# Low parts of the weight strips formed by an accumulating DMA instead of a subtraction on VectorE

## The chip, the cores and the metric

The kernel runs on one core of a Trainium2 chip. The metric is the device time of one execution in microseconds (us), the median of the runs. The core has TensorE (matrix products, PE; its weight loads are listed as PEld), VectorE (DVE), ScalarE (ACT), GpSimd (POOL) and SyncE (SP, which here only issues transfers), and 16 DMA engines that all queues share.

## The reference, cut to what matters

One step of a two-layer network on 512 latent and 128 context tokens with 1024 features, in float32. Layer 0 mixes by differential attention and a spatial gate, layer 1 by a gated convolution; after each mixer stands a squared-ReLU MLP with 4096 hidden features, and a layer norm follows every block. For this change one formula is enough:

```python
def sq_relu_mlp(h, w1, w2):
    return jnp.square(jax.nn.relu(h @ w1)) @ w2
```

Every `h @ w` of the model is such a product. The kernel forms each one from split operands: with w = w_hi + w_lo and h = h_hi + h_lo, each part having 12 significant bits, `h @ w` is w_hi h_hi + w_hi h_lo + w_lo h_hi, three passes of the array that add up in float32.

## The kernel before, in words

The activations are kept with features on the 128 partitions and the 640 tokens along the free axis, in two halves of 320 columns. The weights of all large products are cut on the host into 188 strips of 128x1024 float32 (512 KB), in the order of use, in the DRAM tensor `wall`.

`prepare(i)` (lines 84 to 91) brings strip i into shape: SyncE loads it into a staging tile `raw` (four buffers, line 59, shared with the modulation's weights), a tile `w` of two parts is taken from a pool, and `split` (lines 64 to 67) fills it: ScalarE casts the strip to the 12-bit type into part 0 (line 66), VectorE subtracts part 0 from the strip into part 1 (line 67). `split` is also used for activations; those calls are not touched. The tile `w` comes from a pool of four buffers (`w1p`, line 60) in layer 0's mixer; later from this pool and one of three (`w2p`, line 788) in turn, seven in all. `strip()` (line 98) hands out the next strip and calls `prefetch` for the strip three further on (`LOOKAHEAD`, line 42). It also runs some steps of a background generator: sections of the modulation (`mod_section`, line 150; `mod_products`, line 171), whose weights pass through the same staging tiles.

`mm3` (lines 71 to 74) issues the three passes. A strip gives 48 products of 128x128 with 320 columns; in the token-major projections (`token_major`, line 385) two strips together give 120 products of 256 columns, and the strip is there the moving operand, so its low part is read by the second product. The strips in order: 0 to 3 queries and keys of two heads, used at the start tile by tile as the input arrives; 4 to 7 values (token-major); 8 to 11 queries and keys; 12 to 15 the gate; 16 to 19 the gate's values (token-major); 20 to 27 the output projection; 28 to 91 the MLP; 92 to 123 layer 1's mixer; 124 to 187 its MLP. `run_block` (line 700) uses strips one by one ("alt") or, where a norm follows or precedes, six strips with the first half of the tokens and then the same six with the second ("ab").

The order of the instructions on each engine is made when the program is built: a planner replays the program with a table of costs, and puts each instruction in its engine's queue when, by that table, its inputs and a buffer are there. On the chip each queue runs strictly in that order, and semaphores do the waiting. GpSimd has in all eleven instructions in the trace, all of them clears of tiles; two of them come late, `minus_mean` (line 797) and `zb` (line 1038), each taking memory that earlier tiles give up.

Of the kernel before, what the change touches and what calls it, by code (L numbers as in the profile page):

```python
"""One inference step of the hybrid backbone on one core.

Everything on the chip is kept feature-major ([feature on partitions, token on the free axis]),
512 latent tokens then 128 context tokens, so that products chain without transposes, the adaLN
terms are per-partition scalars and the depthwise convolution slides along the free axis.

Float32 products: each operand is split exactly into hi + lo of 12 significant bits (float32r), and
hi*hi + hi*lo + lo*hi are three passes of the array that accumulate in float32 in PSUM.
"""
# [12 lines left out]
ALU = mybir.AluOpType  # L22
AX = mybir.AxisListType
PSUM = bass.MemoryType.PSUM

P = 128
# [16 lines left out]
AHEAD = 36  # products of the out projection before the spatial gating, which they then alternate with  # L43
WARM = (10, 18, 12)
# The attention's pieces in the order in which they are issued. By two blocks of queries: a, b the
# softmax of each, V the values; by head: C, X the same for the context, N the norm's scales, M the
# norm; F half a strip of the projections.
# [5 lines left out]
def build(ctx, tc, io):  # L53
# [9 lines left out]
    # ---------------------------------------------------------------- helpers  # L63
    def split(hl, src):
        """hl[:, 0] = hi, hl[:, 1] = lo of src (a float32 tile in SBUF)."""
        S.copy(out=hl[:, 0], in_=src)  # L66
        V.tensor_tensor(out=hl[:, 1], in0=src, in1=hl[:, 0].bitcast(F32), op=ALU.subtract)  # L67
# [3 lines left out]
    def mm3(ps, lhs, rhs, first, last):  # L71
        """ps += lhs.T @ rhs; lhs(i), rhs(i) give part i (0 hi, 1 lo)."""
        for n, (i, j) in enumerate(PASSES):
            nc.tensor.matmul(ps, lhs(i), rhs(j), start=first and n == 0, stop=last and n == 2)  # L74

    # ------------------------------------------------- the stream of weights
# [7 lines left out]
    def prepare(i):  # L84
        raw = raw_tile()
        stream["dma"] = nc.sync.dma_start(out=raw, in_=io["wall"][i])
        pool = wpools[stream["slot"] % len(wpools)]
        stream["slot"] += 1
        w = pool.tile([P, 2, D], F32R, name="w")
        split(w, raw)  # L90
        stream["w"][i] = w
# [6 lines left out]
    def strip(ahead=True, behind=None):  # L98
        """The next strip; loads those ahead, and a round of the background, behind the instruction given."""
        i = stream["next"]  # L100
        stream["next"] += 1
        if ahead:
            prefetch(i + LOOKAHEAD)
        with nullcontext() if behind is None else tc.issue_after(behind.ins):
            step_background()
        return stream["w"].pop(i)

    # -------------------------------------------------------------- constants
# [10 lines left out]
    def start_load(out, in_):  # L119
        """The loads that the start needs, in this order."""  # L120
        with in_turn():
            start_dma.append(nc.sync.dma_start(out=out, in_=in_))
# [11 lines left out]
    # ------------------------------------------------------------------ adaLN  # L134
# [5 lines left out]
    # [stream, section, tile]; sections: shift, scale + 1, gate, twice  # L140
# [9 lines left out]
    def mod_section(layer, sec, ps, rows):  # L150
        """A section of a layer's modulation for both streams: KT steps and a last one."""
        for k in range(KT):
            raw = raw_tile()
            nc.sync.dma_start(out=raw, in_=io[f"wmod{layer}"][k * P:(k + 1) * P, sec * D:(sec + 1) * D])
            for b in range(2):
                j = 2 * (k % 2) + b
                nc.tensor.matmul(ps[32 * j:32 * j + 32, :], cs[:, k, :], raw[:, b * 512:(b + 1) * 512],  # L157
                                 start=k < 2, stop=k >= KT - 2)
            yield
        msb = rows()  # L160
        S.copy(out=msb, in_=ps)
        p2 = ps[:, 0:16].rearrange("p (f i) -> p f i", f=4)
        for f in range(4):
            nc.tensor.matmul(p2[:, f, :], msb[:, f * P:(f + 1) * P], sel, start=True, stop=True)
        pv = p2.rearrange("p f (b i) -> p b f i", b=2)
        mod_finish([(modT[layer][:, i, sec, :].rearrange("p (b f) -> p b f", b=2), pv[:, :, :, i],
                     bmod[layer][:, sec * KT:(sec + 1) * KT].rearrange("p (b f) -> p b f", b=2), sec in (1, 4))
                    for i in range(2)])
        yield

    def mod_products(layer, sec, rows):
        """A section of a layer's modulation on VectorE, from the transposed weights: KT steps."""
# [21 lines left out]
    def behind(gen, rate):  # L194
        """Run rate steps of gen with every strip that is fetched."""
        background.append([gen, rate])
# [20 lines left out]
    def mod_products_start(raws, ps):  # L217
        """A feature tile of layer 0's first shift and scale: four partial sums, for both streams."""
# [5 lines left out]
    def mod_finish_start(f, ps, rows):  # L224
        """Their sum, features on partitions."""
# [8 lines left out]
    # The input of a block: x * (1 + scale) + shift, split.  # L234
    def modulate(hl, x, sc, sh, segs, tmp_pool, c0):
        """hl[:, :, cols] from x (its columns start at c0); sc(i), sh(i): [P, 1] by stream."""
# [10 lines left out]
    # =================================================== phase 1: mixer of layer 0  # L247
# [15 lines left out]
    # The start: q and k of two heads, tile by tile as the modulation's weights arrive.  # L263
# [39 lines left out]
    with tc.manual_schedule(engines={mybir.EngineType.PE}):  # L303
        start_ps[3, 0] = mmp.tile([P, HALF], F32, name="mm")

        def keep_warm(n):
            """Products that nobody reads, while there are no others: the array's clock falls when it idles."""
            for _ in range(n):
                nc.tensor.matmul(start_ps[3, 0][:, 0:P], mean_w, mean_w, start=True, stop=True)  # L309
# [39 lines left out]
    def proj_halves(w):  # L349
        """One 128-feature strip over all tokens: the two halves' PSUM tiles, in turn."""  # L350
# [14 lines left out]
    def rotary(kind, h, f):  # L365
        """The rotary on the latent columns, split."""
# [18 lines left out]
    def token_major(consume, tile_, between=None):  # L385
        """[128 tokens, 256 features] for the five token tiles, twice; strips: k quadruples."""
# [24 lines left out]
    def softmax_pair(q, k, qc, kc, nkeys):  # L411
        """(p1 - lam p2) * 2^-E for 128 queries (columns qc) over keys kc..kc+nkeys."""
# [34 lines left out]
    def values(h, pair, es):  # L447
        """The head's values for two blocks of queries."""
# [20 lines left out]
    def context_values(h, e):  # L469
        """The same for the context's queries, which attend to the context's keys alone."""  # L470
# [10 lines left out]
    def attention_scales(h):  # L481
        """RMS norm over the head's 128 features: each token's -2 / sqrt(mean square + EPS)."""
# [30 lines left out]
    def g_consume(t, block, ps):  # L513
        """Layer norm within each group, per token."""
# [38 lines left out]
    # lambda, and a power of two that keeps the attention's output in range  # L553
# [55 lines left out]
    def gates(tag, width):  # L609
        """Two of u's strips, kept in float32."""  # L610
# [7 lines left out]
    def fillers():  # L618
        """Products that run while a softmax does."""
# [40 lines left out]
    def mm_tile(shape):  # L660
        """A bank for products, of the six in turn."""
# [10 lines left out]
    def accumulate(m, half, ps, gt, scale_x=False):  # L672
        """xa += gate * ps (the first time for layer 0: alpha * xa + gate * ps)."""
# [17 lines left out]
    def products(w, nk, srcs, half, m0=0):  # L691
        """Strip w's product with srcs for one half of the tokens."""
# [7 lines left out]
    def run_block(items, order, norm=None):  # L700
        """Strips and what is done with them by half; 'alt' strip by strip, 'ab' one half first. Then norms of a half."""
# [16 lines left out]
    # --- out projection of layer 0: attention's features, then the gated ones  # L718
# [22 lines left out]
    def oa_steps():  # L741
        """The first strips of the projection, product by product."""
# [13 lines left out]
    # spatial gating: mix each 128-token chunk along its tokens, between the projection's products  # L756
# [30 lines left out]
    # ======================================================= phase 2: the rest  # L787
# [12 lines left out]
    # parameters that a norm's outputs are formed with  # L800
    def norm_params(layer, which):
        """alpha * (g, b) for the residual; g', b' for the next block's input."""
# [14 lines left out]
    def rsqrt(v):  # L817
        """-2 / sqrt(v + EPS)."""
# [14 lines left out]
    def tally(m, half):  # L833
        """Moments of xa's half about the mean of its first two tiles, which is taken off xa, tile by tile."""
# [44 lines left out]
    def final_norm(half, pr):  # L879
        """The last norm, from the moments."""  # L880
# [42 lines left out]
    def layer_norm(half, pr, hs):  # L923
        """Norm over the features of xa's half; xa <- residual, hs[k] <- next input, split."""
# [25 lines left out]
    def norms(layer, which):  # L950
        """The next block's input, what normalizes a half into it, and what completes the residual."""
# [25 lines left out]
    def ff(layer, hs, residual, following, then=None):  # L977
        """Squared-ReLU MLP of a layer, from hs into xa; residual() completes xa."""
# [56 lines left out]
    # --- layer 1's mixer: y = W_out(b * conv3(c * x))  # L1035
# [64 lines left out]
# ---- host side: layouts only  # L1100
def _strip(w, m):
    """[p, k, c] of a 1024-row matrix's 128-column block m."""
# [118 lines left out]
```

## Time and profile before

| | |
|---|---|
| runs | 1494.41 and 1495.93 us, median 1495.17 us |
| profiled execution, first to last instruction (span) | 1490.6 us |
| its own time | not listed apart from the span; the runs lie 3.8 to 5.3 us above it |
| TensorE busy | 1477.9 us (99%) |
| VectorE busy | 894.6 us (60%) |
| ScalarE busy | 558.2 us (37%) |
| GpSimd busy | 2.2 us |
| DMA | 161.85 MB, 109 GB/s in the mean |

How to read it: busy time is the union of an engine's instructions; the share is of the span. A busy TensorE is pipelined work, one product of 320 columns starting every 148 ns (624.8 us for 4224). "Waited" is idle time of an engine in front of an instruction, put down to what released it last.

### The profile page before, as it was taken

What the parts mean: (1) busy time and instruction counts of PE and PEld (TensorE: products, weight loads), DVE (VectorE), ACT (ScalarE), POOL (GpSimd) and SP (SyncE); (2) the same over time, 40 slices, a digit from 0 to 9 for tenths busy, and PEclk for the clock granted to TensorE, in tenths of its full rate; (3) what the DMA queues carried; (4) which work ended last, traced back from release to release, by engine and by line L of the source; (5) the groups of instructions that cost most, each with busy time, mean ns of one, the idle gap of its engine ahead of it and who ended that gap; (6) DMA issues with size and microseconds to landing.
All of it is one profiled execution on the core that took longest, in us unless ns stands there. A gap on an engine that the chain in (4) does not pass through costs nothing.

```text
span 1490.6 us, 24292 instructions
## 1 busy us (share of the span) xinstructions
PE 1477.9 (99%) x10126; PEld 1426.1 (96%) x10126; DVE 894.6 (60%) x1726; ACT 558.2 (37%) x1032; POOL 2.2 (0%) x11
## 2 busy tenths in 40 slices
PE   8999999999999999999999999999999999999998
PEld 7779888999999999999999999999999999999997
DVE  3656855789986596586557534449533433433456
ACT  3435655346613213213317522216712312312313
POOL 0000000000000000000000000000000000000000
PEclk9999999999999999999999999999999999999999
DMA  9762015322664274275211322212222222222102
GB/s 353 197 206 78 31 36 199 112 88 71 211 227 142 85 226 142 78 222 154 86 54 59 102 83 71 80 35 86 86 85 73 83 71 71 85 72 71 58 1 71
DMA packets 50877, 161.85 MB, mean 109 GB/s; under 512 B 8400, under 2 KB 12112, under 8 KB 50640
## 3 DMA queue, kind: packets, MB, share of 16 engines
q1 hardware_dynamic: 50768, 160.31, 33.9%
q8 instruction: 79, 1.29, 0.4%
q14 instruction: 30, 0.25, 0.0%
HBM read 157.13 MB, written 3.15 MB: 108 GB/s over the span
## 4 chain that ended last, share of the span: by engine, by line
PE 95%; DVE 2%; DMA 1%; ACT 1%; issue 0%; SPq 0%; ACTq 0%; DVEq 0%
PE mm L74 86%; PE sc L425 2%; PE mod L157 1%; PE po L74 1%; PE mm L751 1%; DMA raw<-wmod 1%; PE pt L459 1%; PE ms L221 1%; PE mm L309 0%; PE st L940 0%; DVE w L67 0%; DMA mraw<-wstart 0%; PE ss L488 0%; PE rb L504 0%; PE st L927 0%
## 5 line engine op out<-in xcount | busy, mean ns | idle before, releaser
L74 PE MATMUL mm<-hn,w 128*128 128x320 f32 x4224 | 624.8, 310 | 0.5 <-ACT hn L241 0.5
L74 PEld LDWEIGHTS mm<-hn,w 128*128 128x128 f32 x4224 | 620.4, 188 | 2.9 <-ACT hn L241 1.7
L74 PE MATMUL mm<-hid,w 128*128 128x320 f32 x3072 | 453.4, 309 | 0.0
L74 PEld LDWEIGHTS mm<-hid,w 128*128 128x128 f32 x3072 | 451.2, 188 | 0.5
L66 ACT CAST w<-raw 128x1024 fp32r<-128x1024 f32 x188 | 196.6, 1047 | 368.6 <-PE mm L74 283.5
L67 DVE TENSOR_TENSOR w<-raw,w 128x1024 fp32r<-128x1024 f32 x188 | 229.4, 1222 | 172.2 <-ACT w L66 170.9
L677 DVE SCALAR_TENSOR_TENSOR xa<-mm,modT,xa 128x128 f32<-128x128 f32 (+2 forms) x264 | 108.0, 435 | 152.5 <-PE mm L74 152.4
L989 ACT ACTIVATE relu<-mm 128x320 f32<-128x320 f32 x128 | 55.7, 436 | 236.3 <-PE mm L74 236.3
L74 PE MATMUL mm<-hin,w 128*128 128x320 f32 x576 | 97.7, 315 | 0.3 <-DVE w L67 0.2
L991 DVE TENSOR_TENSOR relu<-relu,mm 128x320 f32<-128x320 f32 x128 | 61.5, 483 | 54.9 <-ACT hid L990 54.9
L74 PEld LDWEIGHTS mm<-hin,w 128*128 128x128 f32 x576 | 85.1, 188 | 6.1 <-issue 4.3
L178 DVE SCALAR_TENSOR_TENSOR unused<-raw,srows 128x1024 bf16<-128x1024 f32 x56 | 68.4, 1221 | 33.2 <-DMA raw<-wmodT 33.1
L74 PEld LDWEIGHTS mm<-w,hin 128*128 128x128 f32 x480 | 59.4, 190 | 16.7 <-issue 15.2
L178 DVE SCALAR_TENSOR_TENSOR raw<-raw,srows 128x1024 f32<-128x1024 f32 x56 | 68.2, 1219 | 0.5
L74 PE MATMUL mm<-w,hin 128*128 128x256 f32 x480 | 65.6, 288 | 0.4 <-DVE w L67 0.4
L992 DVE TENSOR_TENSOR hid<-relu,hid 128x320 fp32r<-128x320 f32 x128 | 62.5, 491 | 3.2
L990 ACT ACTIVATE hid<-relu 128x320 fp32r<-128x320 f32 x128 | 60.2, 472 | 2.0
L74 PE MATMUL mm<-mx,w 128*128 128x320 f32 x384 | 57.5, 310 | 0.0
L74 PEld LDWEIGHTS mm<-mx,w 128*128 128x128 f32 x384 | 56.5, 188 | 0.5 <-DVE mx L67 0.2
L74 PE MATMUL mm<-mix,w 128*128 128x320 f32 x288 | 43.2, 311 | 0.0
L74 PEld LDWEIGHTS mm<-mix,w 128*128 128x128 f32 x288 | 42.5, 188 | 0.3
L240 ACT ACTIVATE hf<-xa,np 128x192 f32<-128x192 f32 (+1 forms) x72 | 36.8, 560 | 4.5 <-DVE xa L944 4.2
(218 smaller groups left out, 937.0 us busy)
## 6 DMA issues: line engine op xcount, KB each, us to landing
raw<-wall SPq DMA_DIRECT2D x188, 512.0 KB, 3.6
raw<-wmodT SPq DMA_DIRECT2D x56, 512.0 KB, 3.7
raw<-wmod SPq DMA_DIRECT2D x24, 512.0 KB, 5.2
mraw<-wstart SPq DMA_DIRECT2D x16, 512.0 KB, 10.6
x<-xT SPq DMA_DIRECT2D x4, 640.0 KB, 10.0
xa<-xT SPq DMA_DIRECT2D x8, 320.0 KB, 4.5
yT<-xa SPq DMA_DIRECT2D x8, 320.0 KB, 2.3
srows<-silu_rows SPq DMA_DIRECT2D x1, 1024.0 KB
```

The lines of the kernel that those rows point to most:

```text
L66: S.copy(out=hl[:, 0], in_=src)
L67: V.tensor_tensor(out=hl[:, 1], in0=src, in1=hl[:, 0].bitcast(F32), op=ALU.subtract)
L74: nc.tensor.matmul(ps, lhs(i), rhs(j), start=first and n == 0, stop=last and n == 2)
L157: nc.tensor.matmul(ps[32 * j:32 * j + 32, :], cs[:, k, :], raw[:, b * 512:(b + 1) * 512], start=k < 2, stop=k >= KT - 2)
L178: V.scalar_tensor_tensor(out=out, in0=raw, scalar=1.0, in1=rows[:, i], op0=ALU.mult, op1=ALU.mult, accum_out=modT[layer][:, i, sec, f:f + 1])
L240: S.activation(out=hf[:, a - lo:b - lo], in_=x[:, a - c0:b - c0], func=AF.Identity, scale=sc(i), bias=sh(i))
L425: nc.tensor.matmul(scs[i][:, b, 0:n], q[r, x, qc:qc + P], k[r, y, kc + b * n:kc + (b + 1) * n], start=m == 0, stop=m == 2)
L677: V.scalar_tensor_tensor(out=xa[:, m, a:b], in0=ps[:, a - COLS[half][0]:b - COLS[half][0]], scalar=gt(i), in1=xa[:, m, a:b], op0=ALU.mult, ...
L989: S.activation(out=r, in_=ps, func=AF.Relu)
L990: evac.append(S.activation(out=hid[m][:, 0, c0:c1], in_=r, func=AF.Square))
L991: V.tensor_tensor(out=r, in0=r, in1=ps, op=ALU.mult)
L992: lows[0] = V.tensor_tensor(out=hid[m][:, 1, c0:c1], in0=r, in1=hid[m][:, 0, c0:c1].bitcast(F32), op=ALU.subtract)
```

## The change

For the strips from 4 on, `prepare` no longer calls `split`. ScalarE writes the cast of the strip into part 0 as before, and then the strip times -1, cast in the same way, into part 1: the negated high part. Then GpSimd issues a DMA that reads the strip a second time from DRAM and adds it onto part 1, which leaves strip - high part, the low part. The first four strips keep the old form.

```diff
         w = pool.tile([P, 2, D], F32R, name="w")
-        split(w, raw)
+        if i < 4:
+            split(w, raw)
+        else:
+            S.copy(out=w[:, 0], in_=raw)
+            S.mul(out=w[:, 1], in_=raw, mul=-1.0)
+            G.dma_start(out=w[:, 1], in_=io["wall"][i], accum_op=ALU.add)
         stream["w"][i] = w
```

The rest of the diff takes away comments and texts only.

## Rows read from the trace of the kernel before

**Rows 1.** Busy times of the whole run: us, share of the span, instructions.
```profile
PE 1477.9 (99%) x10126; PEld 1426.1 (96%) x10126; DVE 894.6 (60%) x1726; ACT 558.2 (37%) x1032; POOL 2.2 (0%) x11
```

**Rows 2.** Windows: us; PE, PEld, DVE, ACT, POOL busy (instructions); PEclk, DMA share, GB/s.
```profile
300.00:400.00 100.00, 99.48 (x667) 98.02 (x666) 92.50 (x184) 60.33 (x114) 0.00 (x0) 1.00 0.34 107
...
400.00:740.00 340.00, 340.00 (x2320) 340.00 (x2319) 243.39 (x437) 91.41 (x146) 0.00 (x0) 1.00 0.50 154
740.00:1480.00 740.00, 740.00 (x5001) 734.72 (x5000) 366.87 (x628) 250.68 (x432) 1.21 (x2) 1.00 0.22 70
...
1200.00:1300.00 100.00, 100.00 (x684) 100.00 (x683) 38.62 (x63) 26.47 (x42) 0.00 (x0) 1.00 0.23 74
```

**Rows 3.** Timeline at 1200 us: start us, length us, engine, line, what [idle before <-releaser].
```profile
1200.19 1.05 ACT L66 CAST w<-raw 128x1024 fp32r<-128x1024 f32 x1 [5.30 <-PE mm L74]
...
1201.27 1.23 DVE L67 TENSOR_TENSOR w<-raw,w 128x1024 fp32r<-128x1024 f32 x1 [0.41 <-ACT w L66]
...
1207.23 1.05 ACT L66 CAST w<-raw 128x1024 fp32r<-128x1024 f32 x1 [5.99 <-PE mm L74]
```

**Rows 4.** Windows, tile `w` alone: PE, PEld, DVE, ACT (instructions), clock, DMA.
```profile
0.00:231.00 231.00, 133.92 (x841) 117.88 (x841) 24.25 (x20) 20.92 (x20) 1.00 0.46 147
0.00:740.00 740.00, 627.66 (x4166) 603.43 (x4167) 110.74 (x91) 95.08 (x91) 1.00 0.46 147
0.00:1200.00 1200.00, 1084.19 (x7249) 1056.20 (x7250) 189.00 (x155) 162.10 (x155) 1.00 0.38 120
```

**Rows 5.** Waits, whole run: who waited for whom, us in total, times, longest us.
```profile
PE mm L74 <- DVE w L67: 0.6, 2, 0.4
...
PEld mm L74 <- DVE w L67: 1.9, 3, 0.8
...
SPq L86 <- DVE w L67: 797.7, 144, 26.2
```

**Rows 6.** Groups: busy us, mean ns of one | idle us before, releasers.
```profile
L66 ACT CAST w<-raw 128x1024 fp32r<-128x1024 f32 x188 | 196.6, 1047 | 368.6 <-PE mm L74 283.5
L67 DVE TENSOR_TENSOR w<-raw,w 128x1024 fp32r<-128x1024 f32 x188 | 229.4, 1222 | 172.2 <-ACT w L66 170.9
...
L676 ACT ACTIVATE xa<-xa 128x320 f32<-128x320 f32 x8 | 3.7, 464 | 1.9 <-DMA xa<-xT 1.9
```

**Rows 7.** DMA issues: count, KB each, median us from issue to landing.
```profile
raw<-wall SPq DMA_DIRECT2D x188, 512.0 KB, 3.6
...
mraw<-wstart SPq DMA_DIRECT2D x16, 512.0 KB, 10.6
```

**Rows 8.** Timeline about 55 us: strips 4 and 5, and the products that use them.
```profile
53.27 1.05 ACT L66 CAST w<-raw 128x1024 fp32r<-128x1024 f32 x1
...
54.85 1.07 ACT L66 CAST w<-raw 128x1024 fp32r<-128x1024 f32 x1
...
55.79 0.43 SPq L86 DMA_DIRECT2D raw<-wall  x1
...
57.09 0.28 PE L74 MATMUL mm<-w,hin 128*128 128x256 f32 x1
57.75 2.42 PE L74 MATMUL mm<-w,hin 128*128 128x256 f32 x18 [0.38 <-DVE w L67]
```

**Rows 9.** Timeline about 295 us: products of strip 22 on, casts of strips 25 to 27.
```profile
293.74 18.50 PE L74 MATMUL mm<-mix,w 128*128 128x320 f32 x125
293.94 1.05 ACT L66 CAST w<-raw 128x1024 fp32r<-128x1024 f32 x1 [10.03 <-PE mm L751]
...
297.96 1.05 ACT L66 CAST w<-raw 128x1024 fp32r<-128x1024 f32 x1
...
299.93 1.06 ACT L66 CAST w<-raw 128x1024 fp32r<-128x1024 f32 x1 [0.93 <-DVE mix L67]
```

**Rows 10.** GpSimd's two late instructions, whole run.
```profile
231.15 0.21 POOL L797 MEMSET minus_mean<- 128x128 f32 x1 [229.79 <-DVE mix L67]
741.16 1.21 POOL L1038 MEMSET zb<- 128x643 f32 x2 [509.81 <-DVE raw L178]
```

## The prediction

> **What bounds the kernel now.** I read busy time first, then the stretches, then the waits, then single instructions. In the busy times TensorE is busy for 1477.9 of 1490.6 us [rows 1], so all its idle time together is 12.7 us, 0.85% of the span. In the windows it is busy for over 99% of every stretch shown, at granted clock 1.00, the higher level of 2.4 GHz [rows 2]. So nothing that this change touches can be worth much on the fast side: it can only take away idle time of TensorE, or add some.
>
> The strips come in faster than they are used. A strip is 48 matmuls. In the stretch at 1200 us the high-part cast starts every 7.04 us (1200.19, 1207.23), each time after ScalarE had waited over 5 us for a TensorE product [rows 3]: the cast waits for a buffer that TensorE has just finished reading, so the buffers are full. Counting up to 1200 us, 7249 products have read strips, of which 96 are the excess of the eight token strips (60 instead of 48), so (7249-96)/48 = 149 strips are used up while VectorE has formed 155 low parts [rows 4]: six strips lie ready, about 6 x 7.04 - 2.5 = 39 us of lead. At 740 us it is (4166-96)/48 = 84.8 against 91, again six; at 231 us, with only four buffers and half of the token strips behind, (841-48)/48 = 16.5 against 20, 3.5 strips. TensorE's waits say the same from the other side: for the low parts it waited 0.6 us as a matmul and 1.9 us as a weight load in the whole run [rows 5].
>
> **The change part by part.** 188 strips pass through line 90; strips 0 to 3 keep the old form, so 184 change.
>
> Removed: 184 subtractions on VectorE at 1222 ns [rows 6], 225 us of its 894.6. TensorE waited 2.5 us for them in all. Of this the matmul's 0.38 us at 57.75 [rows 8], with the weight load in front of it about 1 us, belongs to strip 4, which stands below; at most 1.5 us is left to win.
>
> Added on ScalarE: 184 multiplications by -1 of 128x1024. Not in the trace; the cast of the same size takes 1047 ns, and a multiplication of 128x320 takes 464 ns [rows 6], close to a cast or copy of its width. I take 1.05 us each, 193 us, so ScalarE goes from 558 to about 751 us, half of the span. What lies in front of it: in the fullest stretch shown it is at 60% [rows 2], and the some 14 strips of 100 us add 15. It delays chains in the attention (strips 4 to 19) by up to 1.05 us each, 17 us if each one reached TensorE; but VectorE, which is in the same chains, loses 1.22 us each, so -4 to +8 us are the ends and 0 is the value.
>
> Added on DMA: 184 transfers of 512 KB from GpSimd's queue. The trace has neither an accumulating transfer nor any transfer from that queue. Its latency T from issue to landing is bounded below by the median of the same strip loaded by SyncE, 3.6 us, and above by the median of the 512 KB loads of the crowded start, 10.6 us [rows 7]; I take 6 us, nearer to the first, since it moves the same strip but must also read what it adds to. The low part of a strip then stands 1.05 + T = 7 us after its high part, where it stood 1.3 us (1201.24 to 1202.50) [rows 3] to 3.4 us (54.32 to at most 57.75, strip 4) [rows 8] after it.
>
> The Trainium skill, "DMA: Bandwidth & Descriptors", section "Anatomy of one DMA — SWDGE (gpsimd) path", fits such a transfer as about 2.0 us plus its bytes at 436 GB/s, by estimate 3.2 us here; that fit is for a copy, and no run here shows it yet. By it the loss at the strips 4 and 5 below would be 2.0 us instead of 4.8.
>
> Where this lies on the path: with 39 us of lead, nowhere in the steady stages. It shows where a strip is used soon after its buffer comes free.
>
> Strips 4 and 5, at the first products of the values. Their casts start at 53.27 and 54.85 us, and TensorE starts on strip 4 at 57.09 and already waits for its low part, until 57.75 [rows 8]. Strip 5 is the 13th product of a tile, 57.75 + 11 x 0.134 = 59.2 us. After the change: cast to 54.3, multiplication to 55.4 for strip 4; for strip 5 cast to 56.9, multiplication to 58.0, landing 58.0 + T = 64.0. TensorE runs its products in the order written, so it is late by 64.0 - 59.2 = 4.8 us (2.4 with T = 3.6, 9.4 with T = 10.6). Queued behind are only TensorE's own later products; GpSimd has nothing else to do there.
>
> Strips 25 to 27, in the output projection, where six strips are used in one half and only four buffers exist. The products start at 293.74 and a half strip is 24 x 0.148 = 3.53 us, so strips 25, 26, 27 are needed at 304.3, 307.8, 311.4; their casts start at 293.94, 297.96, 299.93 [rows 9]. With the multiplication right behind, T may be 8.3, 7.7 and 9 us before TensorE waits. At T = 6 it costs nothing, at 10.6 some 3 us, not added up because each strip's delay covers the next.
>
> The loads. SyncE's queue waited 797.7 us for VectorE's subtraction, 144 times [rows 5]; this is the staging buffer coming free. It is now freed by ScalarE, somewhat earlier in the dense stages; the loads move earlier by a microsecond or two, which the lead makes worthless. GpSimd's queue: two clears wait there, until 231.15 and 741.16 us [rows 10], and an accumulating transfer put behind one waits with it. Around both, three and six strips lie ready [rows 4], over 20 and 39 us, so zero; if the planner puts a clear earlier than it can run, it costs the part of that time beyond the lead.
>
> Sum against the profiled execution: 1490.6 + 4.8 - 1.5 + 0 = 1493.9 us of span. The runs' median lies 1495.17 - 1490.6 = 4.6 us above the span, for what stands around it; so 1498.5 us.
>
> **The rivals.**
>
> Slower, the 16 DMA engines fill. The stretch from 1200 to 1300 us shows what a plain strip costs: share 0.23 with one strip each 7.04 us, 1.62 us of all engines. From 400 to 740 us the second layer's modulation is loaded beside the strips and the share is 0.50 [rows 2]. Let an accumulating strip cost m plain ones. Then that stage needs 0.50 + 0.23 m: full at m = 2.2, and when (0.23 m - 0.5) x 340 us exceeds the 39 us of lead, from m = 2.7, TensorE waits. At m = 3.5 it loses 104 - 39 = 65 us there and, with 0.22 + 0.81 = 1.03 in the 740 us behind, some 20 more: 1580 us; at m = 4 about 1700. For it: the transfer reads the strip, reads its target and writes it. Against it: two reads and one write suggest m about 2, and reads and writes may overlap.
>
> The Trainium skill, same page, section "Rules for kernel authors", says that an accumulating transfer reads its destination and writes it later; no row here shows how long that holds an engine, and m above is bounded by the arithmetic of the rows alone.
>
> Slower, GpSimd or the transfer takes longer than 7.04 us each, one at a time. Then the lead runs out whatever the share; at 9 us it is 184 x 1.96 = 360 us, 1855 us. For it: the trace has no transfer issued by GpSimd, so its time per issue is unbounded here. Against it: a SyncE issue takes 0.43 us when nothing blocks it [rows 8], a sixteenth of the 7.04 us that a strip has.
>
> No loss at the start: the planner puts other ready products (scores, modulation) ahead of strip 4's, and only the 1.5 us of waits go: 1493 to 1494 us. For it: both kinds of products run in that stretch anyway. Against it: the before kernel already waited there.
>
> The change cannot be 2% faster: that is 30 us, and TensorE idles for 12.7.
>
> **How the numbers follow.** Hidden but for the start, 1498.5 us: 0.63, own range 1491 to 1512 (T from 3.6 to 10.6 gives -2.4 to +4.6 and 3 more, ScalarE -4 to +8, not all at once). No loss at the start: 0.10. DMA engines full: 0.20. Serial transfers: 0.07. The range goes from 1490 to 1560 us: it takes in the first two, and the engine rival up to about m = 3.3, and leaves out less than 0.2. About 2% is what counts as a difference here (1465 to 1525 us is no change). Slower by over 2% needs m above 3.0 or the serial case: 0.17 + 0.07 = 0.24; faster 0.01; the rest, 0.75, within.
>
> **What would show it.** Right: VectorE near 670 us and ScalarE near 751; 184 activations of about 1.05 us on the new line; about 96 MB from a second queue; a gap of TensorE of 2 to 9 us about 57 to 64 us whose releaser is that transfer; TensorE's full busy time from 70 us on; DMA share in 400 to 740 us below 1. Wrong: gaps of TensorE spread over 400 to 740 us with the share at 1 (engines full), a regular period above 7.04 us in the last stages (serial), or a lead at 1200 us below six strips.

## The result, and the profile after

The changed kernel takes 1538.68 us (two runs, 1538.54 and 1538.83), the kernel before 1495.17 us; the ratio is 1.0303 [1.0285, 1.0320] (these two medians alone give 1.0291, 43.5 us). The time lies in the range that was given, but not near the likeliest value of 1498.5 us. Its profiled execution spans 1536.7 us, 46.1 more than the profiled one before.

The page of after, busy times and the two DMA queues (packets, MB, share of the 16 engines):

```profile
PE 1492.6 (97%) x10126; PEld 1437.3 (94%) x10126; DVE 692.1 (45%) x1542; ACT 726.2 (47%) x1216; POOL 161.4 (11%) x195
...
q0 software_dynamic: 26496, 96.48, 34.2%
q1 hardware_dynamic: 50768, 160.31, 33.0%
```

The first line splits the loss. TensorE's idle time is 1536.7 - 1492.6 = 44.1 us, where it was 12.7 [rows 1]: +31.4. Its busy time is 14.7 us longer with the same 10,126 products; most of that is products at half the clock (below). The two add up to the 46.1 us. VectorE (692) and ScalarE (726) came out near the 670 and 751 that the working had; neither is the bound.

The changed lines by groups (line, engine, what, busy us, mean ns | idle before), and the DMA issues (KB each, median us from issue to landing). The lines of the change are 93 to 95 here, and later lines stand five further on:

```profile
L94 ACT ACTIVATE w<-raw 128x1024 fp32r<-128x1024 f32 x184 | 193.3, 1053 | 0.0
L93 ACT CAST w<-raw 128x1024 fp32r<-128x1024 f32 x184 | 192.3, 1045 | 339.2 <-PE mm L74 165.6 <-DMA raw<-wall 132.7 <-issue 30.5
L95 POOL DMA_DIRECT2D w<-wall x184 | 159.2, 865 | 1317.8 <-ACT w L94 1084.1 <-DVE s L374 54.9 <-PE sc L430 52.9
```
```profile
raw<-wall SPq DMA_DIRECT2D x188, 512.0 KB, 4.7
w<-wall POOLq DMA_DIRECT2D x184, 512.0 KB, 7.2
raw<-wmodT SPq DMA_DIRECT2D x56, 512.0 KB, 5.4
raw<-wmod SPq DMA_DIRECT2D x24, 512.0 KB, 7.4
```

The multiplication takes 1053 ns, as estimated. The new transfer lands after 7.2 us in the median (6 was taken), and beside it the others land later too: plain strips after 4.7 us for 3.6 [rows 7], the modulation's two kinds of loads after 5.4 us for 3.7 and 7.4 us for 5.2. One accumulating strip holds the engines for 34.2% of 1536.7 us over 184, which is 2.86 us; a plain strip 1.62 by [rows 2]. That is m = 1.8, below the 2.7 from which the engine rival would bite.

Where the loss lies, by windows of after (us; busy of PE, PEld, DVE, ACT, POOL; granted clock, DMA share, GB/s):

```profile
0.00:100.00 100.00, 85.89 (x628) 68.48 (x628) 37.26 (x94) 41.55 (x72) 5.29 (x13) 0.95 0.80 254
300.00:400.00 100.00, 94.44 (x627) 92.08 (x626) 73.05 (x164) 59.55 (x102) 11.44 (x14) 0.98 0.63 155
400.00:760.00 360.00, 344.96 (x2313) 343.38 (x2312) 197.11 (x404) 145.01 (x212) 43.21 (x50) 0.99 0.84 223
800.00:1450.00 650.00, 650.00 (x4411) 647.65 (x4410) 209.28 (x432) 310.62 (x477) 78.64 (x91) 1.00 0.67 148
```

These three stretches lose, and 800 to 1450 us loses nothing, with the full 650 us busy. In the first 100 us TensorE was busy for 94.4 us before:

```profile
0.00:100.00 100.00, 94.41 (x717) 74.99 (x717) 52.69 (x118) 41.63 (x74) 0.83 (x8) 1.00 0.79 257
```

In 300 to 400 us the idle time was 0.5 us and is 5.6; in 400 to 760, where before TensorE was busy throughout the 340 us shown [rows 2], it is 15.0, at a DMA share of 0.84 that is not full. How much each stage loses is read from where the same products start in the traces of before and after. The first product of strip 22 (line 74, `mm<-mix,w`) starts at 311.74 us where it started at 293.74: 18.0 us are lost up to there. The first product of layer 0's MLP (`mm<-hn,w`) starts at 362.18 for 337.71, so the output projection loses 6.5 us. The last product of that MLP (`mm<-hid,w`) starts at 838.93 for 792.37: 22.1 us. What follows takes 0.5 us less.

The lead of the strips is as it was. Counting up to 1200 us:

```profile
0.00:1200.00 1200.00, 1050.06 (x6938) 1020.22 (x6939) 4.79 (x4) 298.09 (x294) 125.14 (x145) 0.99 0.70 180
```

With four old-form strips and 145 transfers, 149 low parts are issued, and (6938 - 96)/48 = 142.5 strips are used up: still six ahead, as in [rows 4]. So running out of strips is not what happens in the middle. TensorE's waits say what does (who waited for what: us, times, longest):

```profile
PE mm L74 <- DVE relu L996: 11.2, 3, 4.2
PE mm L74 <- DMA w<-wall: 9.2, 2, 4.7
PE mod L162 <- DMA raw<-wmod: 5.8, 5, 3.0
PE mm L74 <- DVE xa L682: 3.8, 3, 1.8
```
```profile
DVE unused L183 <- DMA raw<-wmodT: 126.5, 42, 7.3
```

Only two of the waits are for the new transfer, 9.2 us. VectorE's evacuations (`relu`, `xa`: it reads finished sums out of TensorE's accumulators) hold TensorE for 15 us, and VectorE itself waits 126.5 us for the modulation's weights. The same rows of before, the wait and the landing of these loads:

```profile
DVE unused L178 <- DMA raw<-wmodT: 33.1, 21, 2.8
```
```profile
raw<-wmodT SPq DMA_DIRECT2D x56, 512.0 KB, 3.7
```

The wait has grown fourfold. The three places, in the timeline (start, length, engine, line, what [idle before <-releaser]).

The start, strip 4:

```profile
54.90 1.08 ACT L94 ACTIVATE w<-raw 128x1024 fp32r<-128x1024 f32 x1
...
56.30 1.00 POOL L95 DMA_DIRECT2D w<-wall  x1 [54.93 <-DVE s L374]
...
58.54 0.41 PE L430 MATMUL sc<-k,q 64*128 64x320 f32 x2 [1.01 <-ACT k L66]
...
64.92 3.57 PE L74 MATMUL mm<-w,hin 128*128 128x256 f32 x15 [4.52 <-DMA w<-wall]
```

From issue to release stand 8.6 us. The planner had put twelve products of scores ahead of strip 4's other products; they filled little of the time. Then TensorE waited 4.52 us, and 15 products of 256 columns took 3.57 us, 238 ns each, against 2.42/18 = 134 ns in [rows 8]: half the clock.

The output projection:

```profile
311.94 1.05 ACT L93 CAST w<-raw 128x1024 fp32r<-128x1024 f32 x1 [9.32 <-PE mm L756]
...
316.55 1.05 ACT L93 CAST w<-raw 128x1024 fp32r<-128x1024 f32 x1
...
318.85 0.86 POOL L95 DMA_DIRECT2D w<-wall  x1 [3.53 <-ACT w L94]
...
320.74 0.86 POOL L95 DMA_DIRECT2D w<-wall  x1 [1.02 <-ACT w L94]
...
327.99 6.20 PE L74 MATMUL mm<-mix,w 128*128 128x320 f32 x30 [4.65 <-DMA w<-wall]
```

The transfer issued at 318.85 releases TensorE 9.1 us later. It is strip 25's, although its cast, at 316.55, is the second: from strip 25 on the tiles come from the two pools in turn (line 87), strip 25 and 27 from the new one and strip 26 from the old. The cast at 311.94 waited for the last product of line 756, which gives up strip 21's buffer in the old pool, so it is strip 26's. Its transfer, issued at 314.24, had landed at 323.9 and did not release TensorE, which stood still from 323.3 on.

Four transfers were issued here, at 314.24, 318.85, 320.74 and 322.63 us, and landed 9.7, 9.1, 11.0 and 12.9 us later. The landings stand 3.8 to 4.0 us apart, twice as far as the last three issues, so in such a burst a transfer's time is in part that of those ahead of it.

Layer 0's MLP, one of its gaps:

```profile
618.09 0.48 DVE L996 TENSOR_TENSOR relu<-relu,mm 128x320 f32<-128x320 f32 x1
618.20 0.33 SPq L180 DMA_DIRECT2D raw<-wmodT  x1
624.90 1.23 DVE L183 SCALAR_TENSOR_TENSOR unused<-raw,srows 128x1024 bf16<-128x1024 f32 x1 [5.80 <-DMA raw<-wmodT]
...
626.17 1.22 DVE L183 SCALAR_TENSOR_TENSOR raw<-raw,srows 128x1024 f32<-128x1024 f32 x1
...
627.32 0.48 DVE L996 TENSOR_TENSOR relu<-relu,mm 128x320 f32<-128x320 f32 x1
627.86 5.31 PE L74 MATMUL mm<-hn,w 128*128 128x320 f32 x24 [4.11 <-DVE relu L996]
```

VectorE's queue runs in order. Two products of the modulation stand ahead of the next evacuation, and their weights, asked for at 618.20, are there at 624.90. The evacuation that frees an accumulator for TensorE therefore starts at 627.32, and TensorE has been idle for 4.11 us. No product here waits for a strip. The load itself could not be asked for earlier: it was issued when the VectorE product of 616.94 gave up its staging tile. SyncE's queue waits for such products 31 times, and since each product waits for its own load, one late load can delay the next:

```profile
SPq L180 <- DVE raw L183: 167.2, 31, 13.1
```

Behind the long gaps the clock is at the lower level, 1.2 GHz (windows of after; the clock is the third number from the end):

```profile
62.00:68.00 6.00, 3.08 (x14) 3.08 (x15) 3.02 (x16) 4.90 (x8) 1.73 (x2) 0.50 1.05 257
...
328.30:331.00 2.70, 2.70 (x11) 2.70 (x11) 0.01 (x1) 0.00 (x0) 0.00 (x0) 0.50 1.08 281
509.30:511.70 2.40, 2.15 (x8) 2.15 (x9) 1.57 (x4) 0.44 (x1) 0.00 (x0) 0.50 0.60 167
...
748.00:750.70 2.70, 2.70 (x12) 2.70 (x11) 1.06 (x3) 0.44 (x1) 0.00 (x0) 0.50 0.85 288
```

There are seven such stretches, with 23.2 us of busy time at half the clock in all, half of it more than the same products take at the full clock. That is some 12 of the 14.7 us of longer busy time, about 1.7 us a stretch; the other 3 us are not explained here. Six of the stretches stand at or behind gaps of 2.9 to 4.65 us, so such a gap costs about half as much again. The seventh, at 232 us, has no long gap ahead of it and stays open.

### The profile page after: what moved, and what is told of

It reads as the page before. It is cut to its first block, busy times and chain, and to the rows that moved or that the text cites. A ratio compares the mean times of both kernels' runs of the same rounds, so it can differ in the third digit from the quotient of the medians.

```text
span 1536.7 us, 24640 instructions
## 1 busy us (share of the span) xinstructions
PE 1492.6 (97%) x10126; PEld 1437.3 (94%) x10126; DVE 692.1 (45%) x1542; ACT 726.2 (47%) x1216; POOL 161.4 (11%) x195
## 3 DMA queue, kind: packets, MB, share of 16 engines
q0 software_dynamic: 26496, 96.48, 34.2%
HBM read 253.60 MB, written 3.15 MB: 167 GB/s over the span
## 4 chain that ended last, share of the span: by engine, by line
PE 51%; DMA 2%; DVE 1%; ACT 0%; issue 0%; ACTq 0%; DVEq 0%
PE mm L74 50%; DMA raw<-wmodT 2%; DVE raw L183 0%; DVE unused L183 0%; PE st L945 0%; ACT xa L907 0%; PE st L932 0%; DVE xa L891 0%; PE st L870 0%; PE st L871 0%; DVE xa L900 0%; PE st L875 0%; ACTq L1213 0%; PE st L874 0%; DVE r L830 0%
## 5 line engine op out<-in xcount | busy, mean ns | idle before, releaser
L93 ACT CAST w<-raw 128x1024 fp32r<-128x1024 f32 x184 | 192.3, 1045 | 339.2 <-PE mm L74 165.6
L95 POOL DMA_DIRECT2D w<-wall x184 | 159.2, 865 | 1317.8 <-ACT w L94 1084.1
L94 ACT ACTIVATE w<-raw 128x1024 fp32r<-128x1024 f32 x184 | 193.3, 1053 | 0.0
L183 DVE SCALAR_TENSOR_TENSOR unused<-raw,srows 128x1024 bf16<-128x1024 f32 x56 | 68.5, 1223 | 126.5 <-DMA raw<-wmodT 126.5
```

What stands on the lines that cost most here:

```text
L93: S.copy(out=w[:, 0], in_=raw)
L94: S.mul(out=w[:, 1], in_=raw, mul=-1.0)
L95: G.dma_start(out=w[:, 1], in_=io["wall"][i], accum_op=ALU.add)
L183: V.scalar_tensor_tensor(out=out, in0=raw, scalar=1.0, in1=rows[:, i], op0=ALU.mult, op1=ALU.mult, accum_out=modT[layer][:, i, sec, f:f + 1])
```

## The experiments

Two theories for the loss. Theory 1: the extra traffic makes transfers late, and it costs where a late transfer meets a chain without lead. Theory 2: it is the longer latency of the low part itself, whatever the bytes. Each diff is against the changed kernel unless it says otherwise.

**The transfer cut to 16 KB.**

```diff
-            G.dma_start(out=w[:, 1], in_=io["wall"][i], accum_op=ALU.add)
+            G.dma_start(out=w[:, 1, 0:32], in_=io["wall"][i][:, 0:32], accum_op=ALU.add)
```

> The accumulating transfer adds only the first 32 of the 1024 columns (16 KB instead of 512 KB); the other columns of the low part keep the negated high part. The queues keep the changed kernel's order but for the first products after the start. Theory 1 (traffic: the added bytes make the strips' low parts and the modulation's loads late): the gaps of TensorE about 65 and 328 us and between 480 and 750 us go, VectorE's wait for the modulation's weights falls from 126 us to near the 33 us of before, time 1497 to 1505 us. Rival (order and ScalarE: the planner's new order and the second ScalarE pass make the gaps): the gaps between 480 and 750 us stay, 15 us of them, time 1520 us or more.

1501.80 us, ratio 1.0057 [1.0037, 1.0077]. Layer 0's MLP is whole again, with VectorE waiting 71.3 us for the modulation's weights; near 33 was expected, so the changed order, with no more than these small transfers, already lengthens that wait. What remains is ahead of the MLP: strip 4 still holds TensorE for 3.97 us, which was expected to go, and strip 25 for 0.84 us. The first product of strip 22 starts 8.4 us later than before; 1.7 of these are a stretch at half clock from 8.8 us on, ahead of every changed strip. The MLP's window, and the landing:

```profile
400.00:760.00 360.00, 360.00 (x2457) 360.00 (x2456) 194.74 (x401) 150.35 (x213) 47.25 (x56) 1.00 0.50 152
```
```profile
w<-wall POOLq DMA_DIRECT2D x184, 16.0 KB, 3.6
```

So a thirty-second of the bytes still takes 3.6 us to land. The bytes explain the MLP's loss and most of the output projection's; the gap at strip 4 is there almost without them.

**A copy instead of an addition.**

```diff
-            G.dma_start(out=w[:, 1], in_=io["wall"][i], accum_op=ALU.add)
+            G.dma_start(out=w[:, 1], in_=io["wall"][i])
```

> The same transfer without the addition: part 1 receives the whole strip instead of the low part. All queues are in the same order as in the changed kernel. Theory 1 (traffic, by the engines' time): the share of GpSimd's queue falls from 34% to 17 to 20%, the latency from 7.2 us to 4 to 5, and more than half of the loss goes: 1505 to 1520 us. Rival (a fixed price of a transfer issued by GpSimd, whatever it does): latency stays at 7 us and time at 1535 to 1540 us.

1509.63 us, ratio 1.0110 [1.0089, 1.0130]. The bytes are the same, the time of the engines is about half (18.2% for 34.2%), the landing is 4.6 us and GpSimd's issue 531 ns (865 with the addition):

```profile
q0 software_dynamic: 26496, 96.48, 18.2%
...
w<-wall POOLq DMA_DIRECT2D x184, 512.0 KB, 4.6
```
```profile
400.00:760.00 360.00, 360.00 (x2457) 360.00 (x2456) 201.77 (x416) 155.75 (x227) 28.77 (x54) 1.00 0.69 232
```

At a share of 0.69 the MLP loses nothing, and at 0.84 it loses 15 us; VectorE's wait lies between, at 95.2 us. Strip 4 (3.15 us) and strip 25 in the output projection (2.26 us) still wait. The addition is thus about half of the engines' time and, by the ratios, (3.03 - 1.10)% of 1495 = 29 of the 45 us.

**The old form through layer 0's MLP alone**, strips 28 to 91.

```diff
-        if i < 4:
+        if i < 4 or 28 <= i < 92:
```

> The strips 28 to 91 (layer 0's MLP) are formed the old way, all others from 4 on the new way. Theory 1: the gaps between 480 and 750 us (15 us and three stretches at the lower clock, 5 us) go, the gaps at 65, 70 to 78 and 328 us stay: 1516 to 1522 us. Rival (the 16 engines are too slow for two transfers a strip everywhere, hidden by the lead): new gaps in the later stages, over 1525 us.

1518.23 us, ratio 1.0167 [1.0147, 1.0188]. No gap in 400 to 760 us, VectorE's wait at 32.4 us as before; TensorE's two waits for the new transfer, at the start and in the output projection (9.2 us), stay. Layer 0's MLP is worth (3.03 - 1.67)% = 20 us by the ratios; by the starts of the products it was 22.1 us in the changed kernel, and here it takes as long as before.

**The old form in all of layer 0**, strips up to 91.

```diff
-        if i < 4:
+        if i < 92:
```

> The strips 0 to 91 are formed the old way, only layer 1's 96 strips the new way. Theory 1: nothing is exposed there, 1494 to 1497 us. Rival (each strip costs a little, 43.5 us over 184): 1495 + 96 x 0.24 = 1518 us.

1492.52 us beside 1492.94, ratio 0.9999 [0.9989, 1.0009]. Ninety-six strips go by the new way in layer 1, each landing after 6.7 us, and the time is that of before. VectorE's 96 subtractions that are saved buy nothing either. The windows show both halves:

```profile
400.00:760.00 360.00, 360.00 (x2457) 360.00 (x2456) 251.94 (x454) 94.64 (x150) 2.22 (x3) 1.00 0.49 152
800.00:1450.00 650.00, 650.00 (x4417) 648.31 (x4417) 201.31 (x418) 301.44 (x466) 77.52 (x90) 1.00 0.65 144
```

**The traffic beside the kernel before**, first form; the diff is against the kernel before.

```diff
-        split(w, raw)
+        split(w, raw); i < 4 or G.dma_start(out=extra[i % 4][:, 0:D], in_=io["wall"][i], **({"accum_op": ALU.add} if i > 7 else {}))
```

> The kernel before, every queue but GpSimd's in its order, plus one transfer of GpSimd per strip from 4 on that adds the strip onto one of four scratch tensors in DRAM (the first four copy it), which nobody reads: the traffic alone. Theory 1a (the traffic alone makes the loss of layer 0's MLP): VectorE's wait for the modulation's weights rises from 33 us to 90 or more and gaps of TensorE appear between 400 and 760 us, 1505 to 1520 us. Theory 1b (the traffic costs only in the planner's new order, where VectorE's queue has two modulation products close together): the wait rises but TensorE has no gaps there, 1493 to 1500 us.

1715.73 us, ratio 1.1487 [1.1416, 1.1559]. The design failed: nothing held the transfers back, so they ran far ahead of the strips and kept the engines full until past 600 us (share 1.06 in the windows 0 to 200 and 200 to 400 us, 1.01 in 400 to 640). It says nothing of the traffic as it falls in the changed kernel.

**Without the modulation's loads**, the changed kernel with VectorE's products reading rows that are there.

```diff
-            raw = raw_tile()
-            nc.sync.dma_start(out=raw, in_=io["wmodT"][6 * layer + sec - 5, f])
...
-                V.scalar_tensor_tensor(out=out, in0=raw, scalar=1.0, in1=rows[:, i], op0=ALU.mult, op1=ALU.mult,
+                V.scalar_tensor_tensor(out=out, in0=rows[:, 1 - i], scalar=1.0, in1=rows[:, i], op0=ALU.mult, op1=ALU.mult,
```

> The changed kernel without the 56 loads of modulation weights beside layer 0's MLP; VectorE multiplies rows that are already there, so the second layer's modulation and one gate of the first are not the reference's. Theory 1 (VectorE stands in front of these loads, and TensorE's products wait behind it for their banks): the gaps between 480 and 750 us go with the three low-clock stretches, the others stay, 1516 to 1522 us. Rival (the second ScalarE pass makes the evacuations late): they stay, 1530 us or more.

1514.92 us, ratio 1.0143 [1.0113, 1.0172], a little below what was expected. All gaps of the MLP are gone, though all accumulating transfers run and VectorE has the same products in its queue:

```profile
400.00:760.00 360.00, 360.00 (x2457) 360.00 (x2456) 198.81 (x405) 158.44 (x234) 45.85 (x53) 1.00 0.71 160
```
```profile
PE mm L74 <- DMA w<-wall: 9.3, 2, 4.7
```

The two waits for strips are as in the changed kernel. So the MLP's loss needs the modulation's loads, and the strips' loss doesn't. That leaving them out also takes their own traffic away (share 0.71) is a limit of this run: it shows that the chain is theirs, not at which share they become late.

**The old form up to strip 7, and up to strip 27.**

```diff
-        if i < 4:
+        if i < 8:
```
```diff
-        if i < 4:
+        if i < 28:
```

> The strips 4 to 7, too, are formed the old way. Theory 1 (the start's loss is the latency of the low parts of strips 4 and 5): the gaps between 58 and 78 us and the low clock behind them go, 16 us: 1520 to 1525 us. Rival (it is traffic: the loads of the modulation's weights wait behind accumulating transfers of any strip): at most the 4.5 us gap and its clock go, 1530 us or more.

> The strips 4 to 27, too, are formed the old way: only the two MLPs and layer 1's mixer use the new form. Theory 1: only layer 0's MLP loses, 20 us: 1512 to 1517 us. Rival (the MLP's gaps follow from a stream that is late since the start): they shrink as well, under 1508 us.

The first takes 1529.17 us, ratio 1.0238 [1.0191, 1.0285], the second 1519.61 us, 1.0174 [1.0145, 1.0204]; both are longer than expected, and the MLP lost more here than in the changed kernel. The start's gaps are gone in the first (94.40 us busy in the first 100, as 94.41 before), the output projection's gap as well in the second:

```profile
400.00:760.00 360.00, 340.93 (x2260) 339.30 (x2259) 189.29 (x390) 138.43 (x201) 42.38 (x49) 0.97 0.82 218
```
```profile
300.00:400.00 100.00, 99.86 (x670) 98.52 (x669) 82.63 (x175) 69.98 (x126) 9.65 (x11) 1.00 0.68 177
400.00:760.00 360.00, 343.11 (x2294) 341.14 (x2293) 185.61 (x382) 138.46 (x199) 44.12 (x51) 0.98 0.82 218
```

Idle in the MLP is 19.1 us in the first and 16.9 in the second, with 15.0 in the changed kernel; probably small shifts in time decide which evacuation meets a late load. By the ratios the three parts are 10, 10 and 26 us, but these differences mix in the MLP's change, and the intervals are wide. By the starts of the products, up to strip 22 the first run loses 5.1 us and the second 4.0 (of which 3.4 us are a stretch at half clock from 8.6 us on, ahead of every changed strip), where the changed kernel loses 18.0; the output projection loses 6.4 and nothing, the MLP 28.2 and 23.4. So strips 4 to 7 are worth 12.9 us, the output projection 6.5, and the some 5 us of strips 8 to 21 are not traced further.

**The traffic beside the kernel before**, paced: each transfer waits for its strip's low part. The diff is against the kernel before.

```diff
+    def paced(i, w):
+        after = G.tensor_copy(out=tiny, in_=w[:, 1, 0:1].bitcast(F32))
+        with tc.issue_after(after.ins):
+            G.dma_start(out=extra[i % 4][:, 0:D], in_=io["wall"][i], **({"accum_op": ALU.add} if i > 7 else {}))
...
-        split(w, raw)
+        split(w, raw); i < 4 or paced(i, w)
```

> The kernel before, with VectorE's subtractions kept, and beside them one transfer of 512 KB per strip from GpSimd's queue that nothing reads: it adds the strip onto a scratch tensor in DRAM (the first four of them copy). A copy of one column of the strip's low part, on GpSimd, goes ahead of each, so a transfer starts only when its strip's low part stands, and the order of the other engines is that of the kernel before. This gives the traffic without any product depending on it. Theory 1a (the traffic alone makes layer 0's MLP late): VectorE's wait for the modulation's weights rises from 33 us to 90 or more, TensorE has gaps between 400 and 760 us as in the changed kernel, 1505 to 1520 us. Theory 1b (the traffic needs the changed order of VectorE's work to hurt): the wait rises, but TensorE stays without gaps there, 1493 to 1500 us.

1509.84 us, ratio 1.0118 [1.0101, 1.0135]. The traffic is that of the changed kernel (96.48 MB, 34.4%, share 0.84 in the MLP), and no product of a strip depends on it:

```profile
400.00:760.00 360.00, 350.87 (x2374) 349.32 (x2373) 250.21 (x452) 94.49 (x152) 60.67 (x106) 1.00 0.84 224
```
```profile
PE mm L74 <- DVE relu L998: 7.0, 4, 3.6
...
PE mm L74 <- DVE xa L684: 1.1, 1, 1.1
```
```profile
DVE unused L185 <- DMA raw<-wmodT: 67.7, 27, 6.2
```

Both expectations are half right: the time is in the range of 1a, but VectorE's wait, 67.7 us, stays below the 90 of it. With the order of the kernel before, the traffic alone makes 9.1 us of idle time in the MLP, nearly all by the same evacuations, so the changed order isn't needed for a loss; but there are 15 to 19 us where the planner's new order also stands, and VectorE waits 126.5 us there. By the starts of the products the MLP loses 12.2 us here for 22.1. The scratch tensors are in DRAM and the transfer lands a little later (8.3 us), and VectorE keeps its subtractions, so the split between traffic and order is not exact.

## Why the prediction was right or wrong

**The range** holds the measured time by luck. It reached to 1560 us for engines that fill, at up to m = 3.3, and they didn't. The mechanism that was held likeliest, hidden but for the start, had its own range of 1491 to 1512 us, and the time lies 27 us above that; the 46.1 us come by other ways.

**Right.** The sign of the risk, and what bounds the kernel: nothing was to be won (96 subtractions less, ratio 0.9999). The multiplications cost 1053 ns and are hidden. GpSimd's two late clears run at 314.78 and 786.82 us and cost nothing [rows 10]; SyncE's queue waits 731.7 us for the multiplication where it waited 797.7 for the subtraction [rows 5], also for nothing. In the middle stages no strip came late and six lay ready. Serial transfers of over 7.04 us each didn't occur: a transfer lands after 7.2 us, but in the burst of the output projection one landed every 3.8 to 4.0 us. The engines didn't fill: m is 1.8, and the 0.50 + 0.23 m of the working gives 0.91 for a measured 0.84.

**The start**: the mechanism was right, its size not. The working had TensorE late by 4.8 us; the gap on the transfer is 4.52 us, but it is strip 4's, at a T of 8.6 us, and not strip 5's at 6, so that the two numbers are close is luck. Beside it stand 1.5 us of waits for the scores that the planner had put ahead, 4.8 us for modulation weights (0.9 before, 0.6 with transfers of 16 KB), and two stretches at half clock. With the old form up to strip 7 the long gaps go, and with them 12.9 us, over twice the term. The term for ScalarE's second pass in the attention was put at 0 within -4 to +8 us; some 5 us are lost at strips 8 to 21, and no run separates that pass from the planner's order there.

**Strips 25 to 27**: "at T = 6 it costs nothing, at 10.6 some 3 us". Two things were wrong. The casts at 293.94, 297.96 and 299.93 [rows 9] were read as those of strips 25, 26 and 27; by the pools, the first is strip 26's and the second strip 25's, the one that is needed first. Strip 25 had 304.3 - (297.96 + 2.1) = 4.2 us, not 8.3, and at T = 6 it would have cost 1.8 us. And T was 9.1 us for that transfer: 9.1 - 4.2 = 4.9 for the measured 4.65. The other two runs fit as well: the copy, 6.7 us for this transfer, leaves 2.5 for a measured 2.26, and 16 KB, 4.6 us, 0.4 for 0.84. T was taken as one number near a plain strip's median, while the places without lead are here those where strips are asked for in a burst; there it is 9 to 13 us, at a share of 0.89 (313 to 328 us), and the median of 7.2 tells nothing of it.

**The step that failed** is "with 39 us of lead, nowhere in the steady stages". It measured the lead of the strips and let it stand for all transfers. The modulation's weights share the engines and the staging buffers, and they have no such lead: VectorE already waited for them in the kernel before, 33.1 us in 21 waits of up to 2.8 us, and TensorE had no gap from them. With 1.7 us more from issue to landing in the median (5.4 for 3.7), there are 42 waits of up to 7.3 us, and six of them show as gaps of TensorE, 15 us in all. The engine rival was looked at by the share being full, and the loss came below that. The run without these loads and the run with the traffic alone show this chain. That the remaining 6 to 10 us of idle time in the MLP come from the planner's order is argued from the difference to the latter run, and from VectorE's wait of 71.3 us in the changed order with transfers of 16 KB; no run has the order without any transfer.

**Left out** was the clock. The windows of before were at 1.00, and the working added gaps at their own length. Of the 46.1 us, some 12 are what products at the lower level took longer. The Trainium skill, "TensorE: Matmul & The Clock Gate", section "Part 1: The HAM clock gate (the "warmup" mystery)", says that the array's clock follows how busy the engine has been; the windows here agree where a long gap is ahead (0.50 at 62 to 68, 328, 509 and 748 us), and the stretch at 232 us is left open.

**The last step of the sum** added 4.6 us "for what stands around" the span. In the profiled executions that list both, the time lies 1.7 to 2.1 us above the span (in the changed kernel 1538.54 and 1536.7 us); the rest of the 4.6 us is then the difference between the profiled execution and the two timed runs. The forecast of 1498.5 us does not change by it, as it stands on the median of these runs.

The Trainium skill, "DMA: Bandwidth & Descriptors", section "Anatomy of one DMA — SWDGE (gpsimd) path", has the fit for a transfer on GpSimd's path that the prediction took 3.2 us from, by estimate, for 512 KB. The measurements decide against it here: 4.6 us for the copy and 7.2 with the addition, both beside other traffic.

## What to carry to other kernels

Moving work from a compute engine with slack to the DMA engines adds latency to every other transfer, so look for the stream with the least lead, not for the one that is changed: its rows are the waits of any engine on a DMA, with the longest, and what stands behind the waiting instruction in its queue. Take a transfer's time from the crowded places where nothing is ready ahead, not from the median. Check which buffer an instruction waits for before you name the strip that it belongs to. Price a gap of TensorE of 3 to 5 us at about one and a half times its length, when rows of the same kernel show the clock falling there, as here.

## What was not expected of the hardware

- An accumulating transfer holds the DMA engines 1.9 times as long as a copy of the same bytes from the same queue (34.2% of 1536.7 us against 18.2% of 1506.9, 96.48 MB each), and GpSimd takes 865 ns to issue it against 531.
- A thirty-second of the bytes only halves the landing: 3.6 us for 16 KB, 7.2 for 512 KB, both accumulating, and the small ones also have less traffic beside them. GpSimd's issue of the small one takes as long, 866 ns.
- The idle time in one stage, with the same loads in it, went from nothing at a DMA share of 0.69 (the copy) to 15 us at 0.84, below full.
- Four accumulating transfers of 512 KB issued within 8.4 us landed 3.8 to 4.0 us apart.
